# Top-2 gate and dispatch: the second group's two large loads moved from the sync queue to the scalar queue

## The chip, the cores and the metric

The kernel runs on one core of a Trainium2 chip. The metric is the device time of one execution in microseconds (us); lower is better. Before the change the median of three runs is 239.64 us (239.61 to 239.66).

Five engines appear in the profile. PE does no work here. DVE (VectorE) does the multiplications, ACT (ScalarE) the sigmoids, a few rows and some DMA issues, SP (SyncE) only issues DMAs, and POOL (GpSimd) only fills four constants. A DMA issued by SP goes over the queue that the profile calls q1, one issued by ACT over the queue q10. The data of both queues is moved by the same 16 DMA engines of the core.

## What is computed

For each of 16 x 1024 = 16384 tokens there are 8 router logits and a vector of 512 floats. The two largest softmax probabilities are taken and divided by their sum, and the token's vector is written out twice, once times each of the two weights, the smaller weight first:

```python
probs = exp(router_logits - max); probs /= sum(probs)
topk_indices = argsort(probs)[..., -2:]
topk_probs   = take_along_axis(probs, topk_indices)
topk_probs  /= sum(topk_probs)
out = x[:, :, None, :] * topk_probs[..., None]      # 16 x 1024 x 2 x 512, float32
```

With two experts left, the two weights are sigmoids of plus and minus the difference of the two largest logits, so no softmax over 8 is needed. The input x is 33.6 MB, the output 67.1 MB, the logits 0.5 MB. All bytes have to pass the DMA engines once.

## The kernel before, in words

The tokens lie on 128 partitions, 128 tokens per partition. A "row" in what follows is one token on each of the 128 partitions: 2 KB per partition in x, 4 KB per partition in the output. The 128 rows are cut into two groups of 65 and 63 rows (`GROUPS`).

There are two large buffers in SBUF. `xs` holds up to 65 rows of x, and `osp` holds 18 output rows. Each group is loaded into `xs` in three pieces (`LOADS`: 6, 28 and 31 rows for the first group, 4, 28 and 31 for the second) and written out in pieces (`STORES`). An output piece is computed by one DVE instruction at L164 (two where a piece is cut), which multiplies the loaded rows by the two weights, and then stored by one DMA at L176. Some output pieces are computed into `osp`. Others are computed in place over the rows of `xs` that are no longer needed, because two output rows of 2 KB halves take the room of two rows of x; these are the pieces marked `"xs"`, two per group.

The first group's pieces are 3 rows (early, stored over the scalar queue), 15 rows, 16 rows in `xs` rows 0 to 31, 15 rows, and 16 rows in `xs` rows 33 to 64. The second group's pieces are 16 rows in `osp`, 16 rows in `xs` rows 0 to 31, 15 rows in `osp`, and 16 rows in `xs` rows 32 to 63. The last two rows of the second group's first piece are done by ACT (four `ACTIVATE` at L157), the rest of it by DVE.

The second group's loads overwrite `xs`, so they have to wait for the first group's stores out of `xs`:

- The load of 4 rows goes to `xs` rows 1 to 4. It is issued by ACT. Ahead of it stands the `pause`, a small ACT copy at L128 that is made to wait until the first group's last store but one has landed.
- The load of 28 rows goes to `xs` rows 5 to 32. The rows it overwrites left with the first group's third store, which is long gone by then.
- The load of 31 rows goes to `xs` rows 33 to 63. It overwrites the source of the first group's last store, so its issue waits until that store has landed.

The DVE instruction and the four ACT instructions of the second group's first piece need both the load of 4 rows and the load of 28 rows. The load of 31 rows is first read by the third piece (its cut of two rows).

What sets the order: each engine runs its instructions one after the other, and a waiting instruction holds up what is behind it on the same engine. `tc.keep_in_program_order` ties an instruction behind the one traced just before it on the same engine; all loads and stores and the pause are tied in this way. The other instructions (DVE, and ACT's four `ACTIVATE` at L157) are not tied, and a planner orders them at build time by when it takes them to be ready.

Of the kernel before, what the change touches and what calls it, by code (L numbers as in the profile page):

```python
# [1 line left out]

# [4 lines left out]

F32 = mybir.dt.float32
ALU = mybir.AluOpType
ACTF = mybir.ActivationFunctionType  # L10
P = 128


def top2_weights(nc, WA, dlt, room, logits, E):

    tt = nc.vector.tensor_tensor
    hi, lo, n = None, None, E  # L20
    while n > 1:
        n //= 2
        if hi is None:
            a, b = logits[:, :, 0:n], logits[:, :, n : 2 * n]
            nhi, nlo = room(n), b
            tt(nhi, a, b, op=ALU.max)  # L26
            tt(nlo, a, b, op=ALU.min)  # L27
        else:
            a, b = hi[:, :, 0:n], hi[:, :, n : 2 * n]
            nhi, nlo, tmp = room(n), room(n), room(n)  # L30
            tt(tmp, lo[:, :, 0:n], lo[:, :, n : 2 * n], op=ALU.max)  # L31
            tt(nlo, a, b, op=ALU.min)  # L32
            tt(nlo, nlo, tmp, op=ALU.max)  # L33
            tt(nhi, a, b, op=ALU.max)  # L34
        hi, lo = nhi, nlo
    tt(dlt, hi[:, :, 0], lo[:, :, 0], op=ALU.subtract)  # L36
    nc.scalar.activation(WA[:, :, 0], dlt, ACTF.Sigmoid, scale=-1.0)  # L37
    nc.scalar.activation(WA[:, :, 1], dlt, ACTF.Sigmoid, scale=1.0)  # L38

GROUPS = [65, 63]

LOADS = [[6, 28, 31], [4, 28, 31]]
BASE = [0, 1]

STORES = [
    [(0, 3, "osp", 0), (3, 15, "osp", 3), (18, 16, "xs", 0), (34, 15, "osp", 0), (49, 16, "xs", 33)],
    [(0, 16, "osp", 2), (16, 16, "xs", 0), (32, 15, "osp", 0), (47, 16, "xs", 32)],
]  # L50

L = 18

FREE = [3, 2]

ACT_ROWS = 2


@with_exitstack
def kernel(  # L60
    ctx: ExitStack,
    tc: tile.TileContext,
    x: bass.AP,
    router_logits: bass.AP,
    k: bass.AP,
    out: bass.AP,
):
    nc = tc.nc
    B, S, D = x.shape
    E = router_logits.shape[-1]  # L70
    N = B * S
    assert int(k) == 2 and E == 8 and N == P * sum(GROUPS)
    M = N // P

    x_v, o_v, rl_v = [], [], []
    t0 = 0
    for n in GROUPS:
        t1 = t0 + P * n
        x_v.append(
            x.rearrange("b s d -> (b s) d")[t0:t1].rearrange("(p m) d -> p m d", p=P)  # L80
        )
        o_v.append(
            out.rearrange("b s k d -> (b s) k d")[t0:t1].rearrange(
                "(p m) k d -> p m k d", p=P
            )
        )
        rl_v.append(
            router_logits.rearrange("b s e -> (b s) e")[t0:t1].rearrange(
                "(p m) e -> p m e", p=P
            )  # L90
        )
        t0 = t1

    wpool = ctx.enter_context(tc.tile_pool(name="wpool", bufs=1))
    xs = wpool.tile([P, max(GROUPS), D], F32)
    osp = wpool.tile([P, L, 2, D], F32)
    WA = wpool.tile([P, M, 2], F32)
    dlt = wpool.tile([P, M], F32)


    flat = osp.rearrange("p l k d -> p (l k d)")
    taken = [0]

    def room(n):
        o = taken[0]
        taken[0] += M * n
        return flat[:, o : o + M * n].rearrange("p (m n) -> p m n", n=n)

    logits = room(E)

    def place(where, at, n):

        if where == "osp":
            return osp[:, at : at + n]
        return xs[:, at : at + 2 * n, :].rearrange("p (r k) d -> p r k d", k=2)

    m0 = 0
    stores = []
    for g, G in enumerate(GROUPS):
        x0, r = BASE[g], 0  # L120
        for n in LOADS[g]:

            late = g == 1 and r == 0
            if late:


                rows = xs[:, x0 : x0 + 2, :]
                pause = nc.scalar.activation(rows, rows, ACTF.Copy)  # L128
                tc.add_manual_dep(
                    pause.ins,  # L130
                    stores[-2].ins.name,
                    mybir.DependencyInfo(
                        mybir.DependencyClass.Sync, mybir.DependencyReason.DATA
                    ),
                    reason="begin when the store ahead of the last has landed",
                )
                tc.keep_in_program_order(pause)
            queue = nc.scalar if late else nc.sync
            load = queue.dma_start(xs[:, x0 + r : x0 + r + n, :], x_v[g][:, r : r + n, :])  # L139
            tc.keep_in_program_order(load)  # L140
            r += n
            if g == 0 and r == 6:
                n0 = GROUPS[0]
                tc.keep_in_program_order(nc.sync.dma_start(logits[:, :n0], rl_v[0]))  # L144
                tc.keep_in_program_order(nc.sync.dma_start(logits[:, n0:], rl_v[1]))  # L145
                top2_weights(nc, WA, dlt, room, logits, E)
        assert r == G
        for r, n, where, at in STORES[g]:
            og = place(where, at, n)

            again = where == "osp" and at == 0 and r > 0
            cuts = [0, FREE[g], n] if again else [0, n]
            if g == 1 and r == 0:
                cuts = [0, n - ACT_ROWS]
                for j in range(n - ACT_ROWS, n):
                    for k2 in range(2):
                        nc.scalar.activation(  # L157
                            og[:, j, k2, :],
                            xs[:, x0 + r + j, :],
                            ACTF.Copy,  # L160
                            scale=WA[:, m0 + r + j, k2 : k2 + 1],
                        )
            for a, b in zip(cuts, cuts[1:]):
                nc.vector.tensor_tensor(  # L164
                    og[:, a:b],
                    xs[:, x0 + r + a : x0 + r + b, :]
                    .unsqueeze(2)
                    .to_broadcast([P, b - a, 2, D]),
                    WA[:, m0 + r + a : m0 + r + b, :]
                    .unsqueeze(3)  # L170
                    .to_broadcast([P, b - a, 2, D]),
                    op=ALU.mult,
                )

            queue = nc.scalar if g == r == 0 else nc.sync
            stores.append(queue.dma_start(o_v[g][:, r : r + n], og))  # L176
            tc.keep_in_program_order(stores[-1])
        m0 += G


# [1 line left out]
_INS = ['x', 'router_logits', 'k']  # L182
_OUTS = [((16, 1024, 2, 512), 'float32')]

_NUMBERS = {'k': 2}


# [26 lines left out]
```

## Time and profile before

| what | before |
|---|---|
| median of three runs | 239.64 us |
| time of the profiled execution | 239.64 us |
| its span, first to last instruction | 237.9 us |
| DVE busy | 139.8 us (59%) |
| ACT busy | 5.4 us (2%) |
| DMA bytes | 101.19 MB, mean 425 GB/s |
| queue q1 (issued by SP) | 98.57 MB, 96.2% of the 16 engines' span |
| queue q10 (issued by ACT) | 2.62 MB, 2.6% of the 16 engines' span |

The profiled execution took 239.64 us, the same as the median; 1.7 us of it lie outside the span. Times in the rows are microseconds from the start of the span. "L164" is a line of the kernel. `SPq` and `ACTq` are DMA issues by SP and ACT, and "to landing" is the time from an issue until the data has arrived and the waiting engine may go on. A form such as `out_dram<-osp` names what is written and what is read. An entry in square brackets at the end of a row says how long the engine sat idle before it and what it waited for.

### The profile page before, as it was taken

To read this page: it belongs to the slowest core of one execution; us is meant where nothing else is said; L and a number is where in the kernel's file an instruction comes from. 1 tells how busy PE (TensorE), PEld (TensorE's weight loads), DVE (VectorE), ACT (ScalarE), POOL (GpSimd) and SP (SyncE) were. 2 spreads that over 40 slices of the span, in tenths; PEclk is the share of its full clock that TensorE was granted. 3 is DMA by queue.
4 is the path that set the end of the run, shared out by engine and by line. 5 is a ranking of instruction groups with operands and counts; after the bars stand their busy time and mean duration, and the time that the engine had idled before them with its cause. 6 is when DMAs were issued, how large, how long until landed. Compare 5 with 4: busy or idle time off the path is not lost.

```text
span 237.9 us, 111 instructions
## 1 busy us (share of the span) xinstructions
DVE 139.8 (59%) x22; ACT 5.4 (2%) x8; POOL 0.2 (0%) x4
## 2 busy tenths in 40 slices
DVE  0650499999689999200000009999976999950000
ACT  2000000000000000010000003000000000000000
POOL 0000000000000000000000000000000000000000
DMA  7989998989998989989998999898998989989894
GB/s 266 550 357 481 441 408 375 486 351 496 397 463 353 529 362 465 496 353 415 555 397 350 444 479 470 384 507 364 485 397 386 496 353 507 465 362 518 353 529 176
DMA packets 2448, 101.19 MB, mean 425 GB/s; under 512 B 272, under 2 KB 400, under 8 KB 528
## 3 DMA queue, kind: packets, MB, share of 16 engines
q1 hardware_dynamic: 2160, 98.57, 96.2%
q10 hardware_dynamic: 288, 2.62, 2.6%
HBM read 34.08 MB, written 67.11 MB: 425 GB/s over the span
## 4 chain that ended last, share of the span: by engine, by line
DMA 49%; DVE 39%; SPq 1%; issue 0%; DVEq 0%
DMA xs<-in_x_dram 29%; DVE osp L164 25%; DMA out_dram<-osp 19%; DVE xs L164 14%; SPq L144 0%; SPq L145 0%; SPq L139 0%; SPq L176 0%; DVEq L164 0%
## 5 line engine op out<-in xcount | busy, mean ns | idle before, releaser
L164 DVE TENSOR_TENSOR osp<-xs,WA 128x3072 f32<-128x3072 f32 (+5 forms) x7 | 67.2, 9604 | 63.5 <-DMA xs<-in_x_dram 56.9
L164 DVE TENSOR_TENSOR xs<-xs,WA 128x16384 f32<-128x16384 f32 x4 | 68.9, 17225 | 0.2
L26 DVE TENSOR_TENSOR osp<-osp 128x512 f32<-128x512 f32 x1 | 0.7, 691 | 8.1 <-DMA osp<-in_router_logits_dram 8.1
L157 ACT ACTIVATE osp<-xs,WA 128x512 f32<-128x512 f32 x4 | 2.6, 709 | 37.6 <-DMA xs<-in_x_dram 37.6
L128 ACT ACTIVATE xs<-xs 128x1024 f32<-128x1024 f32 x1 | 1.1, 1056 | 91.1 <-DMA out_dram<-osp 91.1
L37 ACT ACT_TABLE_LOAD x1 | 1.3, 1283 | 0.7 <-PEq L195 0.7
L27 DVE TENSOR_TENSOR osp<-osp 128x512 f32<-128x512 f32 x1 | 0.7, 691 | 0.0
L32 DVE TENSOR_TENSOR osp<-osp 128x256 f32<-128x256 f32 (+1 forms) x2 | 0.7, 352 | 0.0
L34 DVE TENSOR_TENSOR osp<-osp 128x256 f32<-128x256 f32 (+1 forms) x2 | 0.7, 351 | 0.0
L33 DVE TENSOR_TENSOR osp<-osp 128x256 f32<-128x256 f32 (+1 forms) x2 | 0.7, 351 | 0.0
L31 DVE TENSOR_TENSOR osp<-osp 128x256 f32<-128x256 f32 (+1 forms) x2 | 0.7, 350 | 0.0
L37 ACT ACTIVATE WA<-dlt 128x128 f32<-128x128 f32 x1 | 0.3, 315 | 10.0 <-DVE dlt L36 10.0
L36 DVE TENSOR_TENSOR dlt<-osp 128x128 f32<-128x128 f32 x1 | 0.3, 291 | 0.0
L38 ACT ACTIVATE WA<-dlt 128x128 f32<-128x128 f32 x1 | 0.3, 298 | 0.0
L195 POOL MEMSET const-uint8-127<- 128x1 uint8 x1 | 0.1, 102 | 0.0
L195 POOL MEMSET const-bfloat16-1.0<- 128x1 bf16 x1 | 0.1, 101 | 0.0
L195 POOL MEMSET const-float32-0.0<- 128x1 f32 x1 | 0.1, 98 | 0.2 <-issue 0.2
L195 POOL MEMSET const-float32-1.0<- 128x1 f32 x1 | 0.1, 98 | 0.0
## 6 DMA issues: line engine op xcount, KB each, us to landing
out_dram<-osp SPq DMA_DIRECT2D x3, 7680.0 KB, 23.3
xs<-in_x_dram SPq DMA_DIRECT2D x2, 7936.0 KB, 40.7
xs<-in_x_dram SPq DMA_DIRECT2D x2, 7168.0 KB, 35.1
xs<-in_x_dram SPq DMA_DIRECT2D x1, 1536.0 KB, 5.9
out_dram<-osp ACTq DMA_DIRECT2D x1, 1536.0 KB, 24.8
xs<-in_x_dram ACTq DMA_DIRECT2D x1, 1024.0 KB, 24.8
osp<-in_router_logits_dram SPq DMA_DIRECT2D x1, 260.0 KB, 6.2
osp<-in_router_logits_dram SPq DMA_DIRECT2D x1, 252.0 KB, 6.3
```

The source lines that it names most:

```text
L26: tt(nhi, a, b, op=ALU.max)
L27: tt(nlo, a, b, op=ALU.min)
L31: tt(tmp, lo[:, :, 0:n], lo[:, :, n : 2 * n], op=ALU.max)
L32: tt(nlo, a, b, op=ALU.min)
L33: tt(nlo, nlo, tmp, op=ALU.max)
L34: tt(nhi, a, b, op=ALU.max)
L36: tt(dlt, hi[:, :, 0], lo[:, :, 0], op=ALU.subtract)
L37: nc.scalar.activation(WA[:, :, 0], dlt, ACTF.Sigmoid, scale=-1.0)
L128: pause = nc.scalar.activation(rows, rows, ACTF.Copy)
L157: nc.scalar.activation(og[:, j, k2, :], xs[:, x0 + r + j, :], ACTF.Copy, scale=WA[:, m0 + r + j, k2 : k2 + 1],)
L164: nc.vector.tensor_tensor(og[:, a:b], xs[:, x0 + r + a : x0 + r + b, :] .unsqueeze(2) .to_broadcast([P, b - a, 2, D]), WA[:, m0 + r + a : ...
L195: nc = _bacc.Bacc("TRN2", target_bir_lowering=False, num_devices=1)
```

## The change

One line. The queue of the second group's loads of 28 and 31 rows is the scalar queue and no longer the sync queue. Before, `late` was true only for the second group's first load, the one of 4 rows.

```diff
--- before.py
+++ after.py
@@ -135,7 +135,7 @@
                     reason="begin when the store ahead of the last has landed",
                 )
                 tc.keep_in_program_order(pause)
-            queue = nc.scalar if late else nc.sync
+            queue = nc.scalar if g == 1 else nc.sync
             load = queue.dma_start(xs[:, x0 + r : x0 + r + n, :], x_v[g][:, r : r + n, :])
             tc.keep_in_program_order(load)
             r += n
```

So ACT now issues, one after the other and tied in this order: the pause, the load of 4 rows, the load of 28 rows, the load of 31 rows. SP issues the first group's loads and the stores, apart from the first store of three rows, which ACT issues as before. No piece, byte, buffer or compute instruction changes.

## The prediction

> **What bounds the kernel now.** I read the page's head and its DMA part first, to see which resource is full.
>
> ```profile
> span 237.9 us, 111 instructions
> DVE 139.8 (59%) x22; ACT 5.4 (2%) x8; POOL 0.2 (0%) x4
> DMA  7989998989998989989998999898998989989894
> DMA packets 2448, 101.19 MB, mean 425 GB/s; under 512 B 272, under 2 KB 400, under 8 KB 528
> q1 hardware_dynamic: 2160, 98.57, 96.2%
> q10 hardware_dynamic: 288, 2.62, 2.6%
> ```
>
> The DMA engines are full from end to end: 96.2% + 2.6% = 98.8% of 237.9 us is 235.0 us of work for each of the 16. No compute engine passes 59%. The chain of waits names DVE as well, so I look next at how that chain and the DMA queues fit together in the second half, where the change lies. These are rows of the chain:
>
> ```profile
> 96.78 45.45 DMA xs<-in_x_dram
> ...
> 142.35 15.10 DVE osp L164
> ...
> 157.51 22.79 DMA out_dram<-osp
> ...
> 180.33 14.04 DVE osp L164
> ...
> 194.39 17.23 DVE xs L164
> ```
>
> These are rows of the timeline, with the issues of the same stretch:
>
> ```profile
> 79.13 0.33 SPq L176 DMA_DIRECT2D out_dram<-osp  x1
> 96.39 0.33 SPq L176 DMA_DIRECT2D out_dram<-xs  x1
> 103.62 1.06 ACT L128 ACTIVATE xs<-xs 128x1024 f32<-128x1024 f32 x1 [91.13 <-DMA out_dram<-osp]
> 104.70 0.34 ACTq L139 DMA_DIRECT2D xs<-in_x_dram  x1
> 142.25 2.56 ACT L157 ACTIVATE osp<-xs,WA 128x512 f32<-128x512 f32 x4 [37.57 <-DMA xs<-in_x_dram]
> 174.67 2.29 DVE L164 TENSOR_TENSOR osp<-xs,WA 128x2048 f32<-128x2048 f32 x1
> 180.33 14.03 DVE L164 TENSOR_TENSOR osp<-xs,WA 128x13312 f32<-128x13312 f32 x1 [3.37 <-DMA out_dram<-osp]
> 194.38 0.33 SPq L176 DMA_DIRECT2D out_dram<-osp  x1
> 211.64 0.33 SPq L176 DMA_DIRECT2D out_dram<-xs  x1
> ```
>
> And these are rows of the DMA view, asked for one stretch at a time, so that each row is one transfer (KB where shown, then us from issue to landing): the first group's last store; the second group's loads of 28, 4 and 31 rows; its third store; its last store.
>
> ```profile
> out_dram<-xs SPq DMA_DIRECT2D x1, 28.3
> xs<-in_x_dram SPq DMA_DIRECT2D x1, 7168.0 KB, 45.4
> xs<-in_x_dram ACTq DMA_DIRECT2D x1, 1024.0 KB, 24.8
> xs<-in_x_dram SPq DMA_DIRECT2D x1, 7936.0 KB, 36.2
> out_dram<-osp SPq DMA_DIRECT2D x1, 7680.0 KB, 23.3
> out_dram<-xs SPq DMA_DIRECT2D x1, 25.4
> ```
>
> The transfers land back to back. The first group's store at 79.13 lands at 103.62 (the pause starts then), its last store at 96.39 + 28.3 = 124.7, the load of 28 rows at 96.78 + 45.45 = 142.2. The last two stores land at 194.38 + 23.3 = 217.7 and 211.64 + 25.4 = 237.0. A store of 16 rows is 128 x 16 x 4 KB = 8.39 MB, so the last one alone moved at 8.39 MB in 19.3 us, 434 GB/s. From 103.62 to 237.0 the queues moved one store of 16 rows, 4 + 28 + 31 rows of x and the second group's four stores: 8.39 + 16.52 + 33.03 = 57.94 MB in 133.4 us, which is 434 GB/s again. So the whole stretch that the change touches already runs at the rate of an undisturbed store. There is no hole in it to close, and DVE's place in the chain hides nothing: its last store is issued at 211.64, six microseconds before the store ahead of it has landed.
>
> **The change part by part.** The loads of 28 and 31 rows leave SP's queue and come behind the load of 4 rows in ACT's. The rows for their issues and for SP's wait:
>
> ```profile
> L139 SPq DMA_DIRECT2D xs<-in_x_dram x5: 339/445/953, 0.7 to 124.7; - x5
> SPq L139 <- DMA out_dram<-xs: 26.9, 1, 26.9
> ```
>
> *SP loses two issues* of at most 0.95 us and its wait of 26.9 us. That wait delayed nothing: the next thing on SP is the store at 157.51, and SP was free at 124.7 + 0.95. Gain 0.
>
> *ACT gains two issues*. The load of 28 rows can go at 104.70 + 0.34 = 105.0 instead of 96.78. It was not moving data at 96.78, since the first group's last store lay ahead of it on the same queue until 124.7. The 19.7 us between 105.0 and 124.7 cover the later issue; without that cover it would cost the 8.3 us that the issue is later.
>
> *How the two queues share the engines between 105 and 124.7* decides whether that holds. The load of 4 rows, 1.05 MB, took 24.8 us beside the store. Taken in equal bytes, it would have needed some 2 x 1.05 MB / 434 GB/s = 4.8 us and a start. Taken in turns of one partition's row each (64 KB of the store, 8 KB of the load; eight of each for each of 16 engines), a turn moves 16 x 72 KB in 2.7 us and eight turns take 21.7 us. The row is nearest to that. So the load of 4 rows lasts as long as the store, and the load of 28 rows, behind it, gets its turns only when the store is gone. The bytes moved before the load of 28 rows is complete are the same as now (8.39 + 1.05 + 7.34 MB from 103.62 on), so it lands at 142.2 again. Cost 0.
>
> *ACT now waits* at its issue of the load of 31 rows until the first group's last store lands at 124.7. Behind it on ACT stand the four activations of L157, which need the load of 28 rows and start at 142.25. The wait is over 17.5 us before that, so it costs 0; it would cost from the point at which the store lands later than 142.2. The load of 31 rows is then in the queue 17.5 us before its data can flow, and lands where it does now, at 124.7 + 36.2 = 160.9.
>
> *The second group's first store* is issued at 157.51 on SP, whose queue is now empty, while the load of 31 rows still has 3.4 us to go on ACT's. If they alternate, one or two turns of the load come up to 2 x 2.4 us later (16 x 64 KB at 434 GB/s is 2.4 us): 165.7 at the latest, still ahead of 174.67, when DVE first reads those rows. The store, the longer of the two, ends when the bytes of both are through, at 157.51 + 22.79 = 180.3 as now. Cost 0, unless there is a hole at the change of queues.
>
> That hole no row shows, so I bound it. Below it cannot be less than 0. Above, the slowest start of a queue that has been empty is that of the load of 4 rows. In the stretch from 103 to 110 us the scalar queue shows these packets:
>
> ```profile
> q10 hardware_dynamic: 3, 0.02, 0.8%
> ```
>
> Issued at 104.70, it had moved three packets by 110.0, so the first came some 5.3 us after the issue. As much for the store would be 157.51 + 5.3 = 162.8 against the load's end at 160.9 less a fraction for the landing, 160.5: a hole of 2.3 us. The other end is the very first transfer, with nothing before it. In the first 3 us the DMA row (slices of 0.075 us) is
>
> ```profile
> DMA  0000000000000000000000099995009000979937
> ```
>
> so data flows at 1.73 us, 1.0 us after the issue at 0.7; then the store is ready at 158.5 and the hole is 0. I take 0: the 5.3 us at 104.70 were spent behind rows of the other queue that were already on their way, and here those rows would be the load's own, which keep the engines full.
>
> *The rate with loads on one queue and a store on the other.* From 103.62 to 142.2, with both queues in use for half of it, 16.78 MB took 38.6 us: 435 GB/s, no loss. The nearest row with a loss is the first group, where the early store of three rows on ACT's queue ran beside the loads of 28 and 31 rows:
>
> ```profile
> xs<-in_x_dram SPq DMA_DIRECT2D x1, 7936.0 KB, 45.2
> ...
> xs<-in_x_dram SPq DMA_DIRECT2D x1, 1536.0 KB, 5.9
> osp<-in_router_logits_dram SPq DMA_DIRECT2D x1, 260.0 KB, 6.2
> osp<-in_router_logits_dram SPq DMA_DIRECT2D x1, 252.0 KB, 6.3
> ...
> out_dram<-osp ACTq DMA_DIRECT2D x1, 1536.0 KB, 24.8
> ```
>
> From 0.7 + 5.9 = 6.6 to about 2.7 + 45.2 = 47.9 us (2.7 is about where the third load is issued) went 7.34 + 8.13 + 1.57 + 0.52 = 17.56 MB, 41.3 us against 40.5 at 434 GB/s. Those 0.8 us hold the logits' small packets too. They are the upper end of what mixing can cost; here it lasts one or two turns of eight, so I take 0.
>
> The sum is 0. The profiled execution took 239.64 us, its span of 237.9 and 1.74 around it, which is also the median: forecast 239.65 us.
>
> **The rivals.** *The first: ACT's order.* The four activations of L157 are not tied to their place, and the planner does move instructions:
>
> ```profile
> 9.38 0.42 DVE L32 TENSOR_TENSOR osp<-osp 128x256 f32<-128x256 f32 x1
> 9.72 0.42 DVE L31 TENSOR_TENSOR osp<-osp 128x256 f32<-128x256 f32 x1
> ```
>
> L32 runs ahead of L31. Were the activations put ahead of the load of 31 rows, that load would be issued at 142.25 + 2.56 = 144.8, and the engines, empty from 142.2, would get data 1.0 us later: 3.6 us, 243.3 us in all. It decides as soon as the planner takes the load of 28 rows to land before the first group's last store. The rows speak against it, 142.2 to 124.7, and a planner must be wrong by 17 us.
>
> *The second: the hole* at the change of queues, up to 2.3 us, 241.9 us; against it the reason above.
>
> *The third: mixing costs rate*, up to 0.8 us, 240.4 us; against it the 435 GB/s.
>
> *The fourth: faster.* With the first store on a queue of its own, it could pass the load of 31 rows. At its best it starts at 158.5 and lands after 19.3 us, at 177.8 and not 180.3; DVE's wait of 3.37 us would shrink by 2.5, the last store be issued 2.5 us earlier, and with the landing time of now the kernel would take 237.1 us. Against it: the last store's 25.4 us hold 6 us of waiting behind the store before, so an earlier issue only waits longer. What can be won is idle time of the engines. The span less the first 1.73 us, the 0.9 us after the last landing and the 235.0 us of work leaves 0.3 us: 239.3 us. The Trainium skill (Perfetto Trace Analysis, section DMA Optimizations) advises separate issuing engines for inputs and for outputs, for a more dynamic spread. By that rule this change helps and the 237.1 us stand for it; the trace, at 434 GB/s without a hole, leaves it nothing to spread.
>
> **How the numbers follow.** No change to speak of has 0.81, ACT's order 0.06, the hole 0.06, mixing 0.03, faster 0.04. About 0.2%, 0.48 us, is what a measurement of this kernel can tell from no change. That gives faster 0.04, within 0.2% 0.82 (a little of the hole and of mixing are within it), slower 0.14. The range goes from 239.3, the idle time that can be won, to 240.4, the whole loss by mixing; it leaves out ACT's order, the greater part of the hole and the gain by passing, somewhat over 1 in 10.
>
> **What would show it.** Right: q10 with some 18 MB and q1 with some 83 (15.5 MB moved), the load of 28 rows issued by ACT near 105 and landing near 142.2, the load of 31 rows issued on ACT near 124.7, the first store of the second group landing near 180.3, SP without its wait of 26.9 us. Wrong: the load of 31 rows issued after the activations near 145 (first rival); slices below the others near 160 (second); an earlier landing of the first group's last store or a later one than 124.7, which would say that the queues do not take turns row by row; a last landing other than 237.0 with the chain the same.

## The result, and the profile after

The changed kernel takes 241.55 us (median of five runs, 241.46 to 242.13) against 239.64 us before: a ratio of 1.0085, 95% interval 1.0070 to 1.0099. It is 1.9 us slower, clearly, and outside the range of the forecast. The profiled execution took 241.59 us with a span of 239.8. Of several kernels below, the one before included, a few executions took one to two us longer than the rest, so medians are compared, and no landing is read from the profile of such an execution.

First the rows of the page after that answer to those shown of before (head, DMA slices, queues):

```profile
span 239.8 us, 114 instructions
DVE 139.8 (58%) x22; ACT 5.4 (2%) x8; POOL 0.2 (0%) x4
DMA  7989998979989897999999979998988989799894
DMA packets 2448, 101.19 MB, mean 422 GB/s; under 512 B 272, under 2 KB 400, under 8 KB 528
q1 hardware_dynamic: 1872, 83.10, 80.8%
q10 hardware_dynamic: 576, 18.09, 17.5%
```

The same bytes, the same busy time on DVE, 15.5 MB moved from q1 to q10 as forecast; only the span is 1.9 us longer. The two queues' shares come to 98.3% of 239.8 us, 235.7 us of work for each engine against 235.0 before: the packets took some 0.7 us longer, and for the rest, over 1 us, the engines stood still somewhere. The timeline of the changed kernel from the landing of the second group's first loads on:

```profile
104.87 20.40 ACTq L139 DMA_DIRECT2D xs<-in_x_dram  x3
142.41 2.56 ACT L157 ACTIVATE osp<-xs,WA 128x512 f32<-128x512 f32 x4 [37.57 <-DMA xs<-in_x_dram]
142.50 15.09 DVE L164 TENSOR_TENSOR osp<-xs,WA 128x14336 f32<-128x14336 f32 x1 [45.99 <-DMA xs<-in_x_dram]
157.67 0.33 SPq L176 DMA_DIRECT2D out_dram<-osp  x1
161.22 2.29 DVE L164 TENSOR_TENSOR osp<-xs,WA 128x2048 f32<-128x2048 f32 x1 [3.62 <-DMA xs<-in_x_dram]
163.42 17.22 DVE L164 TENSOR_TENSOR xs<-xs,WA 128x16384 f32<-128x16384 f32 x1
180.67 0.33 SPq L176 DMA_DIRECT2D out_dram<-xs  x1
181.10 14.03 DVE L164 TENSOR_TENSOR osp<-xs,WA 128x13312 f32<-128x13312 f32 x1 [0.46 <-DMA out_dram<-osp]
```

Everything up to 157.67 is as forecast, with the usual tenth or two of difference from run to run: the three loads are issued by ACT from 104.87 on, the last of them once the first group's last store has landed, and the two of 4 and 28 rows have landed at 142.4. Then comes an instruction in another place. In the kernel before, DVE went from the first piece straight to the 16 rows in `xs`, at 157.53, and did the two rows of the cut afterwards, at 174.67. Now the two rows stand first. They need the load of 31 rows, so DVE waits 3.62 us for it, works 2.29 us, and the 16 rows start at 163.42. Their store is issued at 180.67. Before, the 16 rows and their store stood here:

```profile
157.53 17.23 DVE L164 TENSOR_TENSOR xs<-xs,WA 128x16384 f32<-128x16384 f32 x1
...
174.78 0.34 SPq L176 DMA_DIRECT2D out_dram<-xs  x1
```

The order of DVE's instructions in the two programs, from the first piece of the second group on, differs in one place:

```
 L164 TensorTensor osp<-xs,WA 128x14336
+L164 TensorTensor osp<-xs,WA 128x2048
 L164 TensorTensor xs<-xs,WA 128x16384
-L164 TensorTensor osp<-xs,WA 128x2048
 L164 TensorTensor osp<-xs,WA 128x13312
 L164 TensorTensor xs<-xs,WA 128x16384
```

DVE's instructions are not tied to the order in which they are written, and the planner put the two rows ahead once their load was on the other queue. That no compute instruction changes, as said of the change, is true and says nothing of their order.

What the late store does to the DMA engines is seen in the DMA slices from 176 to 186 us (slices of 0.25 us). A packet here is one partition's part of a transfer, 64 KB of a store of 16 rows, and its whole time is booked where it starts. First the kernel before, then the changed one, each with its count of packets:

```profile
DMA  0006990000000999000000099900000069900000
DMA packets 80, 4.19 MB, mean 419 GB/s; under 512 B 16, under 2 KB 16, under 8 KB 16
```

```profile
DMA  0000069990000000000006900000000990000000
DMA packets 64, 3.15 MB, mean 315 GB/s; under 512 B 16, under 2 KB 16, under 8 KB 16
```

Before, the 16 engines start a new packet of 64 KB each every 2.4 us without a break. After, the last packets of the first store start between 177.25 and 178.25 and so are through by some 180.7, but the next ones start only near 181.5, all 16 within 0.2 us, 0.8 us after the issue at 180.67. The engines had run dry: one round of 16 packets is missing from these 10 us.

### The profile page after: what moved, and what is told of

The parts are those of the page before. It is cut to its first block, busy times and chain, and to the rows that moved or that the text cites. A ratio compares the mean times of both kernels' runs of the same rounds, so it can differ in the third digit from the quotient of the medians.

```text
span 239.8 us, 114 instructions
## 1 busy us (share of the span) xinstructions
DVE 139.8 (58%) x22; ACT 5.4 (2%) x8; POOL 0.2 (0%) x4
## 4 chain that ended last, share of the span: by engine, by line
DMA 55%; DVE 31%; SPq 1%; ACT 0%; issue 0%; ACTq 0%; DVEq 0%
DMA out_dram<-osp 30%; DMA xs<-in_x_dram 26%; DVE osp L164 24%; DVE xs L164 7%; ACT xs L128 0%; SPq L144 0%; SPq L145 0%; SPq L139 0%; ACTq L139 0%; DVEq L164 0%; ACTq L128 0%; SPq L176 0%
## 5 line engine op out<-in xcount | busy, mean ns | idle before, releaser
L32 DVE TENSOR_TENSOR osp<-osp 128x256 f32<-128x256 f32 (+1 forms) x2 | 0.7, 354 | 0.0
L31 DVE TENSOR_TENSOR osp<-osp 128x256 f32<-128x256 f32 (+1 forms) x2 | 0.7, 352 | 0.0
```

## The experiments

Two theories stood against each other. **The order of VectorE (DVE)**: the planner's exchange of two instructions makes the hole, and the queues cost nothing. **The two queues**: loads on one queue and stores on the other cost the time, and DVE's late store would have been hidden.

**DVE's order put back, the loads left on the scalar queue.**

```diff
             for a, b in zip(cuts, cuts[1:]):
-                nc.vector.tensor_tensor(
+                mul = nc.vector.tensor_tensor(
...
                     op=ALU.mult,
                 )
+                if g == 1:
+                    tc.keep_in_program_order(mul)
```

> The changed kernel with VectorE's instructions of the second group tied in program order, so that the cut of two rows comes behind the multiplication of 16 rows in xs, as in the kernel before. Both loads stay on the scalar queue. Theory (the order of VectorE is the cause, the queues cost nothing): 239.6 us, the second store of the second group issued near 174.8 and not 180.7, no empty DMA slices near 181. Rival (loads and stores on two queues cost the time, by the change of queues near 160 or by a lower rate): stays at 241.5 us, whatever VectorE's order is.

Measured: 240.20 us (240.04 to 240.35), beside 239.66 of the kernel before on the same chip; ratio 1.0014, interval 1.0001 to 1.0026. Neither number came out. By the medians, some 1.4 of the 1.9 us are gone with DVE's order and some 0.5 us stay; by the ratio, on which the few longer runs of the kernel before weigh, it is 0.3 us that stay. The rows of this kernel:

```profile
157.52 0.33 SPq L178 DMA_DIRECT2D out_dram<-osp  x1
...
174.79 0.33 SPq L178 DMA_DIRECT2D out_dram<-xs  x1
180.94 14.02 DVE L164 TENSOR_TENSOR osp<-xs,WA 128x13312 f32<-128x13312 f32 x1 [3.97 <-DMA out_dram<-osp]
```

The second store is back at 174.79. But the first store, issued at 157.52 as before (157.51), lands 0.6 us later, at 180.94 and not 180.33. Where it loses them is in the window from 160 to 164 us, in which the first two packets of that store start on each engine. The last number of a row is GB/s; the one before it is the DMA share, the packets' time over that of 16 engines, which passes 1 because a packet's whole time is booked where it starts. (Ahead of them stand the busy times of DVE, ACT and POOL and the clock.) First the kernel before, then this one, then the changed kernel:

```profile
160.00:164.00 4.00, 4.00 (x1) 0.00 (x0) 0.00 (x0) 1.00 1.21 524
```

```profile
160.00:164.00 4.00, 4.00 (x1) 0.00 (x0) 0.00 (x0) 1.00 1.34 524
```

```profile
160.00:164.00 4.00, 2.78 (x2) 0.00 (x0) 0.00 (x0) 1.00 1.31 524
```

The same packets, 524 GB/s in all three, took 1.34 and not 1.21 of 4 us: 0.5 us more per engine (0.4 in the changed kernel). Narrower windows put all of it into the first packet: from 159.5 to 161.5 us the share is 1.48 against 1.21, from 161.5 to 164 it is 0.97 in both. It is the first packet after the change from the scalar queue (the load of 31 rows) to the sync queue (the store).

**The kernel before, with DVE's order of the changed kernel.** All loads stay on the queues of before; the two rows are tied ahead of the 16.

```diff
-            for a, b in zip(cuts, cuts[1:]):
-                nc.vector.tensor_tensor(
+            for a, b in list(zip(cuts, cuts[1:])):
+                if g == 1 and again and a == 0:
+                    continue
+                if g == 1 and where == "xs" and r == 16:
+                    early = nc.vector.tensor_tensor(
+                        osp[:, 0:2],
...
+                        op=ALU.mult,
+                    )
+                    tc.keep_in_program_order(early)
+                mul = nc.vector.tensor_tensor(
...
+                if g == 1:
+                    tc.keep_in_program_order(mul)
```

> The kernel before, all its loads on the queues of before, with VectorE's cut of two rows tied ahead of the multiplication of 16 rows in xs, the order of the changed kernel. Theory (VectorE's order is the cause): 241.5 us, with VectorE idle some 3.5 us until the load of 31 rows lands near 160.9, the second store issued near 180.5 and a hole of some 1.5 to 2 us in the DMA row near 181. Rival (the two queues are the cause): 239.6 us, the later store hidden behind the store ahead of it.

Measured: 241.41 us (241.32 to 241.50); ratio 1.0073, interval 1.0060 to 1.0085.

```profile
157.46 0.34 SPq L192 DMA_DIRECT2D out_dram<-osp  x1
161.01 2.29 DVE L167 TENSOR_TENSOR osp<-xs,WA 128x2048 f32<-128x2048 f32 x1 [3.63 <-DMA xs<-in_x_dram]
163.22 17.22 DVE L178 TENSOR_TENSOR xs<-xs,WA 128x16384 f32<-128x16384 f32 x1
180.35 14.02 DVE L178 TENSOR_TENSOR osp<-xs,WA 128x13312 f32<-128x13312 f32 x1
180.47 0.34 SPq L192 DMA_DIRECT2D out_dram<-xs  x1
```

The order alone, with no load moved, gives 1.75 of the 1.9 us: the wait of 3.63 us, the store at 180.47, and this in the slices from 176 to 186 us, where the last packets of the first store start from 177.0 to 177.5 and the next from 181.25 on, a step of some 4 us where a packet takes 2.4:

```profile
DMA  0000990000000000000009000000000900000000
DMA packets 64, 3.15 MB, mean 315 GB/s; under 512 B 16, under 2 KB 16, under 8 KB 16
```

**The changed kernel without the cut of two rows.** With one multiplication of 15 rows there is nothing to put ahead.

```diff
-            cuts = [0, FREE[g], n] if again else [0, n]
+            cuts = [0, FREE[g], n] if again and g == 0 else [0, n]
```

> The changed kernel without the cut in the second group's third piece: one multiplication of 15 rows, so that there are no two rows to be put ahead. Both loads stay on the scalar queue. Theory: 239.6 us; VectorE then starts 15 rows when the first store lands near 180.3 and is done near 196.5, still ahead of the landing of the second store near 199.6. Rival (the two queues): 241.5 us.

Measured: 240.15 us (240.02 to 240.29); ratio 1.0021, interval 1.0012 to 1.0030. DVE's order is undone in another way, and again 1.4 of the 1.9 us go and 0.5 stay; the first store again lands late:

```profile
180.86 16.16 DVE L164 TENSOR_TENSOR osp<-xs,WA 128x15360 f32<-128x15360 f32 x1 [6.08 <-DMA out_dram<-osp]
```

**The changed kernel with a cut of one row in place of two.**

```diff
-FREE = [3, 2]
+FREE = [3, 1]
```

> The changed kernel with a cut of one row in place of two (third piece cut 1 + 14, not 2 + 13), which shortens the instruction that stands ahead of the 16 rows from 2.29 to some 1.2 us. Theory: the second store is issued 1.07 us earlier, near 179.6, the hole is 1.07 us shorter, and the time is 240.5 us. Rival (the two queues): 241.5 us, not moved by the size of the cut.

Measured: a median of 240.42 us (240.31 to 240.45 in four runs, 241.56 and 242.07 in the two others); ratio 1.0050, interval 1.0028 to 1.0071. The median is 1.1 us under the changed kernel's 241.55, as the shorter instruction ahead of the 16 rows says. The profile is of the run of 242.07 us, so no row of it is read.

These four runs say that DVE's order is the cause of the larger part, and that a second loss of half a microsecond belongs to the queues. The next ones ask what kind of loss that is.

**The first store issued earlier.** DVE's order tied as above, loads on the scalar queue, four rows of the first piece on ACT in place of two.

```diff
-ACT_ROWS = 2
+ACT_ROWS = 4
```

> VectorE's order tied as before and both loads on the scalar queue, and ScalarE takes four rows of the second group's first piece in place of two, so that VectorE's part is 12 rows (some 13.0 us in place of 15.1) and the first store is issued near 155.4 in place of 157.5, 5 us and not 3 us before the load of 31 rows is through. What is left with VectorE's order restored, 0.5 us, is to be split. Theory A (the store reaches its own queue too late to have its first rows fetched while the load's last rows go; it needs some 3 us of lead): 239.7 us, the first store lands near 180.3. Theory B (a change from a load on one queue to a store on the other costs 0.5 us whatever the lead): 240.2 us, the first store lands near 180.9.

Measured: 239.85 us (239.71 to 241.88, 13 runs); ratio 1.0001, interval 0.9988 to 1.0015. With 2.1 us more of lead the median is 0.2 us over the 239.66 of the kernel before, and not 0.5, which speaks for theory A. The profile is of the run of 241.88 us, so the landing of the store cannot be read from it; the store's first packets do not take longer in it (a share of 1.13 for 492 GB/s from 160 to 162 us, the same time per byte as 1.21 for 524).

**Its control: the kernel before with four rows on ACT** (DVE's order tied, all loads on the queues of before, the same edit of `ACT_ROWS`).

> The kernel before with VectorE's order tied and four rows of the first piece on ScalarE, so that the first store is issued near 155.4, with all loads on the queues of before: the control to the run with the earlier store. Theory: 239.65 us, since the engines have no hole there to close. If an earlier first store were a gain by itself, this would be some 239.2 us and the earlier run would have hidden the loss and not removed it.

Measured: 239.97 us (239.67 to 241.58, 12 runs) beside 239.72; ratio 1.0022, interval 1.0005 to 1.0039. An earlier store is no gain by itself, so the earlier run removed the loss and did not only outweigh it. It even costs some 0.2 us, as much as in the run above, though no queue is changed here. The rows show where: in the last packets of the load of 31 rows, not in the store. From 157 to 159 us, first the kernel before, then this one:

```profile
157.00:159.00 2.00, 1.91 (x2) 0.00 (x0) 0.00 (x0) 1.00 1.17 508
```

```profile
157.00:159.00 2.00, 2.00 (x1) 0.00 (x0) 0.00 (x0) 1.00 1.28 508
```

The same packets take 0.2 us longer per engine. By the medians (0.19 and 0.25 us over the kernel before) the queues make no difference between the two kernels with four rows on ACT.

**The first store on the scalar queue too, behind the loads.** DVE's order tied, both loads on the scalar queue.

```diff
-            queue = nc.scalar if g == r == 0 else nc.sync
+            queue = nc.scalar if r == 0 else nc.sync
```

> VectorE's order tied as before, both loads on the scalar queue, and the second group's first store also on the scalar queue, behind the load of 31 rows. The change of queues near 160 us is gone; the next one is from this store to the second store, on the sync queue near 180 us, which is issued some 5 us before its turn. Theory A (a late store): 239.65 us, as the kernel before. Theory B (a change from a load to a store): 239.65 us too, no such change is left. A third reading (any change of queues costs 0.5 us): 240.2 us, with the loss at 180 and not at 160.

Measured: 239.74 us (239.56 to 241.24, 12 runs); ratio 0.9999, interval 0.9981 to 1.0018. Without a change of queues at 160 the loss is gone, although the large loads are still on the scalar queue, and the window from 160 to 164 us reads 1.21 for 524 GB/s again. The change at 180, to a store that was issued well ahead, costs nothing that can be measured; the third reading falls.

**The kernel before with only the first store on the scalar queue** (DVE's order tied, the edit of the run above applied to the kernel before).

> The kernel before with VectorE's order tied, all its loads on the queues of before, and only the second group's first store moved to the scalar queue. Now the load of 31 rows is on the sync queue and the store that follows it, issued near 157.5, on the scalar queue: the change of queues near 160 the other way round. Theory (a store issued some 3 us ahead of its turn loses half a microsecond if it is not on the queue of the transfer before it): 240.2 us, first store landing near 180.9. Rival (the loss belongs to the large loads on the scalar queue): 239.65 us, first store landing near 180.3.

Measured: 240.18 us (239.97 to 240.29, 11 runs) beside 239.72; ratio 1.0013, interval 0.9997 to 1.0029. The interval includes 1; by the medians it is the same half microsecond, and 17 of the 23 runs of the kernel before lie below all eleven of this one. With the queues the other way round the loss stays, so it belongs to the change of queues and not to the scalar queue. The window shows it more clearly, 1.29 against 1.21, 0.3 us per engine:

```profile
160.00:164.00 4.00, 4.00 (x1) 0.00 (x0) 0.00 (x0) 1.00 1.29 524
```

The landing was not at 180.9 as expected but here:

```profile
183.27 14.03 DVE L164 TENSOR_TENSOR osp<-xs,WA 128x13312 f32<-128x13312 f32 x1 [6.34 <-DMA out_dram<-osp]
```

The second store, issued near 174.8 on the other queue, takes turns with the last packets of the first; that had been left out.

**One load moved and not the other.** The prediction rests on queues that take turns, one partition's row (one packet) each. If they do, the order of two loads holds only on one queue.

```diff
-            queue = nc.scalar if late else nc.sync
+            queue = nc.scalar if g == 1 and n != 31 else nc.sync
```

> Only the load of 28 rows goes to the scalar queue, the load of 31 rows stays on the sync queue; VectorE's order is that of the kernel before. Reading of the prediction (queues with work take turns row by row): from 124.7 on the two loads alternate, the load of 28 rows lands near 158 to 159 and not at 142, VectorE's first piece starts and the first store is issued some 17 us later, near 174, the engines are empty from 160.6 to some 175, and the time is some 254 us. Rival (what was issued first goes first): 239.7 us.

Measured: 254.53 us; ratio 1.0613, interval 1.0572 to 1.0655.

```profile
158.84 15.09 DVE L164 TENSOR_TENSOR osp<-xs,WA 128x14336 f32<-128x14336 f32 x1 [62.46 <-DMA xs<-in_x_dram]
174.01 0.33 SPq L176 DMA_DIRECT2D out_dram<-osp  x1
```

The load of 28 rows has landed at 158.8, as worked out from turns, 16.3 us later than in the changed kernel, where the load of 31 rows stands behind it on the same queue, and although it was issued 20 us ahead of it. The working left out two things that nearly cancel. Two packets per engine of this load had moved before the turns began, and its landing waits for one turn more: its last large packets have started by 154.2 us, and the 16 small ones that follow, ahead of the landing, nearly all start from 157.6 on, behind a further packet of the other load. The turns themselves cost nothing: from 130 to 154 us the engines change queues at nearly every packet and move 441 GB/s at a share of 1.02, the same time per byte as in the kernel before (445 at 1.03).

```diff
-            queue = nc.scalar if late else nc.sync
+            queue = nc.scalar if g == 1 and n != 28 else nc.sync
```

> Only the load of 31 rows goes to the scalar queue, the load of 28 rows stays on the sync queue; VectorE's order is that of the changed kernel. By the same reading the loads alternate again: the load of 28 rows lands near 158 to 159, the first store is issued near 174, and the time is some 254 us; VectorE's two rows then wait for nothing, since the load of 31 rows has landed, and cost at most 2.3 us more. Rival (what was issued first goes first, and VectorE's order alone counts): 241.5 us.

Measured: 251.83 us; ratio 1.0501, interval 1.0460 to 1.0541.

```profile
156.44 17.29 DVE L164 TENSOR_TENSOR osp<-xs,WA 128x14336 f32<-128x14336 f32 x2 [60.03 <-DMA xs<-in_x_dram]
171.61 0.33 SPq L176 DMA_DIRECT2D out_dram<-osp  x1
```

Turns again, but the load of 28 rows lands 2.4 us earlier than in the run before, and the time is 2.2 us under what was expected. That is one packet's time, and the traces show where it comes from: from 123 to 130.3 us three packets per engine of this load (2.75 MB on q1) start before any of the load of 31 rows does, where the run before has two. The planner put the two rows of the cut ahead in this kernel too (the 17.29 us are both instructions), but not in the one with only the load of 28 rows moved. So it is the queue of the load of 31 rows that moves the planner.

## Why the prediction was wrong

**The step that failed** is the one that was not taken. The part on the change costed each DMA that moves, each wait and each queue, and summed to 0 on the assumption that all else keeps its order. The rows quoted for the first rival (L32 ahead of L31) showed that the planner exchanges DVE's instructions, and that was applied only to ACT's four activations. The two rows of the cut read the load of 31 rows, whose queue was being changed; they were the first candidate. The prediction counted on DVE first reading those rows at 174.67, as before; it read them at 161.22. Runs: DVE's order alone costs 1.75 us, the queues with DVE's order restored 0.5 us.

**Why the exchange costs what it does** could have been worked out from the rows quoted. The load of 31 rows lands at 160.9, so DVE waits 3.4 us from 157.5 on, and two rows take 2.29 us: the 16 rows and their store come 5.7 us later, at 180.5. The first store has landed at 180.3, nothing else is queued, and the next data comes up to 1.0 us after its issue, as at the start of the kernel (0.8 us in both kernels with the exchange): a hole of more than a microsecond. In the kernel that has only this exchange the store was issued at 180.47 and the loss was 1.75 us. That DVE "hides nothing" was true of the last store, with 6 us to spare; the second store has less, and this was not looked at.

**The hole at the change of queues** was a rival with 0.06, costed from 0 to 2.3 us and taken as 0 on the ground that the load's own rows keep the engines full. The engines were not idle there, but the store's first packets took 0.3 to 0.5 us longer. The term is up to 0.5 us and not 0. With it alone the time is 240.2 us, within the range.

**The two losses do not add up.** 1.75 and 0.5 make 2.25, and the changed kernel loses 1.9. In it the second store's issue, 180.67, decides when data flows again, and the first store's late landing (181.10 against 180.3 before) is taken out of the hole. This follows from the rows of the two traces; no run tries it by itself.

**What held.** Turns of one partition's row each: the two runs with one load moved, and the load of 28 rows landing at 142.4. ACT's wait for the first group's last store cost nothing. ACT's order stayed, so the first rival did not occur. Mixing loads and stores on two queues shows no lower rate: behind the first packet the share is that of the kernel before (0.97 from 161.5 to 164 us). The rival by the Trainium skill (Perfetto Trace Analysis, section DMA Optimizations), separate issuing engines for inputs and outputs, found no gain here: with DVE's order tied it costs up to 0.5 us.

## What to carry to other kernels

A change of a DMA's queue can change the order of compute instructions that nobody touched, where a planner is free to order them: compare the instruction order of both programs before anything is costed, and tie the order of instructions whose place matters. Where DMA engines are full, look for the issue with the least lead over the engines running dry, not at the last one. Transfers that must finish in order belong on one queue, and a store that follows a load closely is best put on that load's queue; issued some 2 us earlier it lost 0.2 us here in place of 0.5.

## What the runs showed of the hardware that was not expected

A store that is issued some 3 us ahead of its turn starts without loss behind a load of its own queue (window share 1.21, on either queue), and loses 0.3 to 0.5 us in its first packet on each engine behind a load of the other queue (1.29 with the store on the scalar queue, 1.34 with it on the sync queue). It is not the change of queues as such: where two loads on two queues take turns, the engines change queues at nearly every packet without loss (441 GB/s at a share of 1.02). In the kernels that lose, the store's queue had nothing ahead of it. With some 2 us more of lead the first packets are not slower, but the last packets of the load ahead take 0.2 us longer, on the same queue too (1.28 against 1.17 of 2 us). Why these packets are slower, a fetch of descriptors or of data, these traces do not show.

Two transfers on two queues share the engines by turns of one packet each, whatever was issued first, and the landing of one waits a turn of the other: a load of 28 rows landed 16.3 us later when the next load went on the other queue.
